# A one-layer decoder step: the order of TensorE's matmuls written by hand in the attention and HGRN2 stages

## The chip, the cores and the metric

The kernel runs on one core of a Trainium2 chip. Its engines are PE (TensorE, matrix products and transposes, which write to eight PSUM banks), DVE (VectorE), ACT (ScalarE), POOL (GpSimd) and SP (SyncE, which here issues transfers); each goes through its own instructions in order and waits on semaphores for the others. The metric is the device time of one execution in microseconds, as the median of several.

## What is computed

One layer for 256 prompt tokens and 8 sample sequences of 4 tokens (288 tokens), width 2048:

```python
sh1, sc1, ga1, sh2, sc2, ga2 = _adaln(c, w_ada, b_ada)      # silu(c) @ w_ada: the modulations
h = _rmsnorm(x, n1) * (1.0 + sc1) + sh1
q, k, v, hq, hk, hi, log_f, hg = _project(h, w_in, qg, kg, lb)
a = _attn_finish(attend(q, k, v, lam), subln_g, lam_init)   # differential attention
o_hg, s_new = _hgrn2(hq, hk, hi, log_f, s0)                 # gated linear recurrence, chunks of 64
m = _hgrn2_finish(o_hg, hg, hg_g)
x = x + ga1 * (jnp.concatenate([a, m], axis=-1) @ w_out)
h2 = _rmsnorm(x, n2) * (1.0 + sc2) + sh2
x = x + ga2 * _hier_moe(h2, ...)                            # 4 groups of 4 experts
```

For the sample tokens `attend` reads a paged cache of 2048 past keys and values for each sequence; for the prompt it is causal attention over 256 tokens. All data is float32.

## The kernel before

The program is one stream of Python that records instructions; a scheduler then puts them in an order on each engine, by what it holds to be ready and by priority. Where the code says `issue_after(first)`, what follows is only kept behind `first`; where it records under `keep_in_program_order`, PE's instructions stay in the order of the code. In the part that this change touches neither binds much, so the scheduler weaves single matmuls of different work into each other.

The work of the stages around the change:

- **Projections** (`by_features`, main at L545 to L552). A job takes one slab of a weight matrix (128 x 1024 values), which ACT rounds into a high part `wh` (L463) and DVE subtracts into a low part `wl` (L464), and multiplies it with the high and low parts of the tokens: 24 matmuls named `pf`, 128 x 288, in two groups of 12 (`mm3`, L467). Each job belongs to a step of `run`. The slabs of `wh` and `wl` are in a small ring.
- **Modulations** (`ada`, L386). A step loads two tiles of w_ada and makes 8 matmuls `pm`, 32 columns wide in the array (128*32), one for each quarter of the bank's partitions; 16 steps make one of the six modulations.
- **Cached attention** (`cache`, L1038), 16 items, each 4 slabs of keys and values of two sequences. Keys are turned (transposes `pkc`, L154, into one PSUM bank, `ck`, bank 5), copied by ACT or DVE in turn (`copy`, L157: tiles `kTc`, L160 and L162, three buffers), multiplied with the queries (`plc`, 128*32), weighed (softmax parts on DVE and ACT), turned (`ppc`), multiplied with the values (`poc`, 128*32), and added up on DVE.
- **HGRN2** for one head pair after the other: a tree of elementwise operations on DVE and ACT makes the tiles `X` (L794 to L799, L845, L848; two buffers) whose small products `pA` on PE give the scores inside a chunk; `near` (L837) copies from PSUM under a mask.
- **Prompt attention** in the stage before: logits `pl`, softmax on DVE and ACT, transposes `pdt`, values `po`, norm, transposes `pot`; the norm of the queries by `pqn`.

The streams are joined by `weave` (L120), which takes from several generators in proportion to their numbers of steps: in the attention stage 20 jobs and M0 = 24 modulation steps; in the stage "mid" 8 jobs, M1 = 8 modulation steps and C1 = 24 cache steps; in the stage "hgrn" H1 = 48 jobs and the other 40 of 64 cache steps; then "late", out projection and experts. `BANKS` names for each stage which PSUM banks a kind of tile takes in turn; `use` switches between them. The steps of `turning` are generators that make 8 transposes each, and `late` is a list of products that are recorded later.

Of the kernel before, what the change touches and what calls it, by code (L numbers as in the profile page):

```python
# [20 lines left out]
KC = 16  # L21
# [20 lines left out]
    "mid": {"pm": [7], "acc": [0, 1], "misc": [3, 4], "ck": [5], "cl": [6], "cp": [2]},  # L42
    "hgrn": {"pm": [7], "acc": [0, 1], "misc": [3, 4], "ck": [5], "cl": [6], "cp": [2]},
# [11 lines left out]
M0 = 24  # L55
M1 = 8
C1 = 24
# [74 lines left out]
class Step:  # L132
    def __init__(self, tc, io):
        self.tc, self.nc, self.io = tc, tc.nc, io
        self.flip = 0
        self.turns, self.nslab, self.nbank = {}, {}, {}
        self.pending, self.once = [], []
        self.in_order = False
# [9 lines left out]
    def mm(self, out, lhsT, rhs, start, stop):  # L148
        m = self.nc.tensor.matmul(out, lhsT=lhsT, rhs=rhs, start=start, stop=stop)  # L149
        return self.tc.keep_in_program_order(m) if self.in_order else m  # L150

    def tr(self, out, in_):
        n = in_.shape[0]
        t = self.nc.tensor.transpose(out, in_, self.ident[0:n, 0:n])  # L154
        return self.tc.keep_in_program_order(t) if self.in_order else t
# [230 lines left out]
    def ada(self, g):  # L386
# [7 lines left out]
        for k in range(KC):  # L394
# [6 lines left out]
            def products(h):  # L401
                for j in range(4):
                    m = self.mm(pm[32 * j:32 * j + 32, 256 * h:256 * h + 256], self.cT[:, k, :],
                                ws[h][:, 256 * j:256 * j + 256], k == 0 and h == 1, False)
                    if j == 0:
                        first = m
                return first
            with self.tc.issue_after(products(1).ins):
                products(0)
# [110 lines left out]
    def by_features(self, wname, blk, src, done):  # L520
# [9 lines left out]
        def make(hs, s, ps):  # L530
# [11 lines left out]
            def main():  # L542
                if s == 0:
                    ps.extend([self.acc("pf0"), self.acc("pf1")])
                for j in range(2):  # L545
                    for k in range(4):
                        kc = s * 4 + k
                        c0 = k * 256 + j * 128
                        self.mm3(ps[j][:, 0:NT], [x[:, c0:c0 + 128] for x in box["p"]],
                                 [hi[:, kc, :], lo[:, kc, :]], kc == 0, kc == KC - 1)  # L550
# [487 lines left out]
    def cache(self):  # L1038
# [7 lines left out]
        late = []  # L1046
        run = {}

# [30 lines left out]
        def turning(pr, s, par, pl):  # L1079


            at = pr * 32 + par * 16 + s * 4
            wk = self.pages("cache_k", (at, at + 1, at + 2, at + 3))
            kT = [None, None]
            for h in range(2):
                kT[h] = self.cc.tile([128, KV, 256], F32, tag="kTc", name="kTc", bufs=KTB)
                for k2 in range(2):
                    t = self.bank("ck", "pkc")
                    for k in range(2):
                        for q in range(2):  # L1090
                            kk = 2 * k2 + k
                            self.tr(t[:, (k * 2 + q) * 128:(k * 2 + q + 1) * 128], wk[h][:, q, kk * 128:(kk + 1) * 128])
                    self.copy(kT[h][:, 2 * k2:2 * k2 + 2, :].rearrange("p k t -> p (k t)"), t)
                yield
                if h == 0:
                    while late:
                        late.pop(0)()

            def products():
                if not pl:  # L1100
                    pl.append(self.bank("cl", "plc"))
                first = None
                for h in (1, 0):
                    for k in range(KV):
                        m = self.mm(pl[0][32 * k:32 * k + 32, h * 256:(h + 1) * 256], self.qB[:, 2 * pr + par, k, :],
                                    kT[h][:, k, :], par == 0 and h == 1, par == 1 and h == 0)
                        first = first or m
                return first
            late.append(products)

        def weigh(pr, s, pl):
# [3 lines left out]
            nc.vector.tensor_tensor_reduce(L, pl[0], self.c("bias"), 1.0, -NEG, OP.add, OP.max, mx)  # L1115
# [9 lines left out]
        def turn(L):  # L1125
            t = self.bank("cp", "ppc")
            for q in range(4):
                self.tr(t[:, q * 128:(q + 1) * 128], L[:, q * 128:(q + 1) * 128])
# [4 lines left out]
        def weighted(pr, s, half, pT, po):  # L1133

            at = pr * 32 + s * 4 + half * 2
            wv = self.pages("cache_v", (at, at + 16, at + 1, at + 17))

            def sums():
                for i in range(2):
                    q = half * 2 + i  # L1140
                    for k in range(KV):
                        r = slice(32 * k, 32 * k + 32)
                        self.mm(po[r, 0:256].rearrange("p (a d) -> p a d", a=2), pT[:, q * 128 + 32 * k:q * 128 + 32 * k + 32],
                                wv[i][:, :, k * 128:(k + 1) * 128], q == 0, q == 3)
            return sums
# [26 lines left out]
        def together(*parts):  # L1172

            first = parts[0]()
            with self.tc.issue_after(first.ins):
                for part in parts[1:]:
                    part()

        items = [(pr, s) for pr in range(NB // 2) for s in range(4)]
        pls = {i: [] for i in range(len(items) + 1)}  # L1180
        state = {}

        def update(i, al, po):
# [585 lines left out]
def body(tc, nc, io, stop=None):  # L1769
# [8 lines left out]
    def some(gen, n):  # L1778
        return islice(gen, n), n
# [112 lines left out]
```

## Time and profile before

| | us |
|---|---|
| median of 3 runs | 1487.66 |
| lowest and highest | 1479.43, 1490.71 |
| the profiled execution | 1485.84 |
| its span | 1483.9 |

The stages as the trace shows them (start of the first and of the last matmul of a kind): the start and early part to 158 us, the attention stage to 312, mid and hgrn with the cached attention to 711, late and the out projection to 942, the experts to the end. A matmul in float32 on small tiles leaves two records, so a count of records can be twice that of the instructions. A row of a timeline is start, length, engine, line, operation, output and input, array tile, shape, and how many records were run together; the length holds the pipeline's tail, so the distance of two starts is the time that a matmul takes from PE.

### The profile page before, as it was taken

How to read it: one execution, taken by the hardware profiler on the slowest of the kernel's cores; microseconds unless marked ns; L12 is line 12 of the kernel's file. 1: busy time of each engine (PE TensorE's matmuls, PEld its weight loads, DVE VectorE, ACT ScalarE, POOL GpSimd, SP SyncE). 2: the span in 40 equal slices, each digit the busy share in tenths (PEclk: the TensorE clock that was granted, in tenths of full speed). 3: DMA queues.
4: the chain of work that ended last, by engine and by line, in shares of the span. 5: the costliest groups of instructions: out<-in, count | busy, mean ns of one | idle time of the engine just before them, and what ended most of it. 6: DMA issues, size and time to landing. Idle time of an engine off the chain costs nothing. (4 is left out here: it accounts for less than half of the span.)

```text
span 1483.9 us, 30120 instructions
## 1 busy us (share of the span) xinstructions
PE 1385.3 (93%) x11808; PEld 933.0 (63%) x11808; DVE 652.4 (44%) x1569; ACT 370.3 (25%) x689; POOL 148.0 (10%) x194
## 2 busy tenths in 40 slices
PE   4889899999999989999989999999999999799997
PEld 3566677767878756887767998563535445353532
DVE  2332464564874456596364444224233241413134
ACT  3222243463443324443223432010000000000000
POOL 2000301110000032000041212001010010101011
PEclk9899999999999998999999999899999999799999
DMA  9999986777878867887989765888999999799997
GB/s 319 369 365 342 348 278 239 232 253 259 254 243 269 277 213 234 265 263 228 345 279 339 264 213 188 294 342 314 398 386 399 392 393 397 284 388 389 399 387 286
DMA packets 240808, 457.25 MB, mean 308 GB/s; under 512 B 17178, under 2 KB 84619, under 8 KB 240395
## 3 DMA queue, kind: packets, MB, share of 16 engines
q1 hardware_dynamic: 171218, 374.60, 70.7%
q10 hardware_dynamic: 66818, 74.10, 15.1%
q0 software_dynamic: 2624, 6.56, 1.4%
q8 instruction: 95, 1.56, 0.4%
q14 instruction: 53, 0.43, 0.1%
HBM read 446.94 MB, written 8.26 MB: 307 GB/s over the span
## 5 line engine op out<-in xcount | busy, mean ns | idle before, releaser
L464 DVE TENSOR_TENSOR wl<-w,wh 128x1024 fp32r<-128x1024 f32 x128 | 157.7, 1232 | 190.1 <-ACT wh L463 189.4
L149 PE MATMUL pf<-hhi,wh 128*128 128x288 f32 x640 | 201.5, 315 | 0.0
L463 ACT CAST wh<-w 128x1024 fp32r<-128x1024 f32 x128 | 133.8, 1046 | 267.9 <-PE pf L149 190.0
L149 PE MATMUL pf<-hlo,wh 128*128 128x288 f32 x640 | 199.5, 312 | 0.0
L149 PE MATMUL pf<-hhi,wl 128*128 128x288 f32 x640 | 198.6, 311 | 0.0
L149 PE MATMUL pm<-w,cT 128*32 128x128 f32 (+1 forms) x2048 | 127.2, 355 | 22.6 <-DMA w<-w_ada 21.9
L149 PEld LDWEIGHTS pf<-hhi,wh 128*128 128x128 f32 x640 | 123.2, 193 | 19.2 <-issue 16.8
L149 PEld LDWEIGHTS pf<-hlo,wh 128*128 128x128 f32 x640 | 123.3, 193 | 10.4 <-issue 9.9
L149 PEld LDWEIGHTS pf<-hhi,wl 128*128 128x128 f32 x640 | 123.3, 193 | 8.3 <-issue 7.8
L149 PE MATMUL pa<-w,hp 128*64 128x512 f32 x512 | 117.0, 612 | 6.5 <-PEq L1721 6.5
L149 PE MATMUL pu<-w,hp 128*64 128x512 f32 x512 | 117.4, 595 | 0.7 <-DMA w<-w_exp_up 0.5
L149 PE MATMUL py<-w,hidT 128*64 128x512 f32 x512 | 114.5, 595 | 1.4 <-DVE hidT L162 0.8
L149 PEld LDWEIGHTS pm<-w,cT 128*32 128x32 f32 x2048 | 60.6, 116 | 63.6 <-DMA w<-w_ada 30.4
L154 PE MATMUL pkc<-cst,w 128*128 128x128 f32 x512 | 88.7, 286 | 8.2 <-DVE kTc L162 7.0
L149 PEld LDWEIGHTS pg<-oh,h 128*128 128x128 f32 x768 | 88.4, 195 | 6.5 <-issue 6.5
L149 PE MATMUL pg<-oh,h 128*128 128x128 f32 x768 | 90.5, 279 | 0.0
L149 PEld LDWEIGHTS pu<-w,hp 128*64 128x64 f32 x512 | 38.6, 137 | 75.4 <-issue 66.8
L149 PEld LDWEIGHTS pa<-w,hp 128*64 128x64 f32 x512 | 36.9, 141 | 77.4 <-issue 71.0
L1289 POOL TENSOR_TENSOR x<-x,gt 128x512 f32<-128x512 f32 x24 | 33.1, 1381 | 518.5 <-DVE gt L1287 516.0
L149 PEld LDWEIGHTS py<-w,hidT 128*64 128x64 f32 x512 | 36.5, 137 | 72.8 <-issue 62.3
L1565 DVE SCALAR_TENSOR_TENSOR sa<-sa,cs,pu 128x512 f32<-128x512 f32 x8 | 6.0, 748 | 172.2 <-PE pu L149 172.2
L149 PE MATMUL pf<-mhi,wh 128*128 128x288 f32 x256 | 79.0, 309 | 0.0
(427 smaller groups left out, 2059.2 us busy)
## 6 DMA issues: line engine op xcount, KB each, us to landing
w<-w_ada SPq DMA_DIRECT2D x192, 512.0 KB, 6.6
w<-w_exp_gate SPq DMA_DIRECT2D x128, 512.0 KB, 10.4
w<-w_exp_up SPq DMA_DIRECT2D x128, 512.0 KB, 9.8
w<-w_exp_down SPq DMA_DIRECT2D x128, 512.0 KB, 10.5
w<-w_in ACTq DMA_DIRECT2D x96, 512.0 KB, 5.7
w<-cache_k SPq DMA_DIRECT2D x128, 256.0 KB, 3.9
w<-cache_v SPq DMA_DIRECT2D x128, 256.0 KB, 4.2
w<-w_out ACTq DMA_DIRECT2D x32, 512.0 KB, 5.3
```

Source lines behind the costliest of these rows:

```text
L149: m = self.nc.tensor.matmul(out, lhsT=lhsT, rhs=rhs, start=start, stop=stop)
L154: t = self.nc.tensor.transpose(out, in_, self.ident[0:n, 0:n])
L463: self.nc.scalar.copy(hi, x)
L464: self.nc.vector.tensor_sub(lo, x, hi.bitcast(F32))
L1289: eng.tensor_add(x, x, t[:, 0:n])
L1565: self.nc.vector.scalar_tensor_tensor(sa, sa, cs, pu, op0=OP.mult, op1=OP.mult)
```

## The change

Recording now has `queued` and `stream`: all matmuls that are recorded under `stream()` are tied to the one before them in one chain without a semaphore, so that PE gets them in the order of the code. The products of the modulations, each group of 12 projections, and every part of the cached attention are recorded so. The cached attention is rewritten in steps of one slab of keys (8 transposes into two banks, 5 and 7), four steps for each of the 16 items and a few behind the last, 69 in all: step 0 has the products of the item before's second half and the second half of sums of the one before that; step 2 the first half of both; steps 1 and 3 turn keys, and step 1 also the weights. The modulations leave the stages "mid" and "hgrn", where bank 7 is now the cache's: M0 is 32 (the attention stage has all of them), C1 is 10, the other 59 steps lie over the 48 jobs. The rings of the cache's pages have 7 buffers from "mid" on.

```diff
-    "mid": {"pm": [7], "acc": [0, 1], "misc": [3, 4], "ck": [5], "cl": [6], "cp": [2]},
-    "hgrn": {"pm": [7], "acc": [0, 1], "misc": [3, 4], "ck": [5], "cl": [6], "cp": [2]},
+    "mid": {"acc": [0, 1], "misc": [3, 4], "ck": [5, 7], "cl": [6], "cp": [2]},
-M0 = 24
-M1 = 8
-C1 = 24
+M0 = 32
+C1 = 10
+    def queued(self, m):
+        if self.in_order:
+            return self.tc.keep_in_program_order(m)
+        if self.streaming:
+            if self.streamed is not None:
+                self.tc.add_manual_dep(m.ins, self.streamed.name, mybir.DependencyInfo(
+                    mybir.DependencyClass.NoSync, mybir.DependencyReason.DATA), reason="streamed")
+            self.streamed = m.ins
+        return m
-            with self.tc.issue_after(products(1).ins):
+            with self.stream():
+                products(1)
                 products(0)
...
                 for j in range(2):
+                    with self.stream():
+                        for k in range(4):
...
+        def turned(w):
+            kT = self.cc.tile([128, KV, 256], F32, tag="kTc", name="kTc", bufs=KTB)
+            ts = [self.bank("ck", "pkc") for _ in range(2)]
+            with self.stream():
+                for k2, t in enumerate(ts):
+                    for k in range(2):
+                        for q in range(2):
+                            kk = 2 * k2 + k
+                            self.tr(t[:, (k * 2 + q) * 128:(k * 2 + q + 1) * 128], w[:, q, kk * 128:(kk + 1) * 128])
+            for k2, t in enumerate(ts):
+                self.copy(kT[:, 2 * k2:2 * k2 + 2, :].rearrange("p k t -> p (k t)"), t)
+            return kT
...
+        for i in range(n + 2):
+            w = keys(i, 0) if i < n else None
+            kT0 = kT1
+            with self.stream():
+                if 1 <= i <= n:
+                    products(i - 1, 1, kT0)
+                if i >= 2:
+                    sums(1, pT[i - 2], po[i - 2], wv[i - 2])
...
+            if i >= 2:
+                update(i - 2)
...
+            if i >= 1:
+                L[i - 1], al[i - 1] = weigh(i - 1)
+            kT0 = [turned(w[0])] if i < n else None
             yield
+            if i < n:
+                kT0.append(turned(w[1]))
+            if i >= 1:
+                pT[i - 1], po[i - 1] = turn(L[i - 1])
+                wv[i - 1] = values(i - 1, 0)
+            yield
+            w = keys(i, 1) if i < n else None
+            with self.stream():
+                if i < n:
+                    products(i, 0, kT0)
+                if i >= 1:
+                    sums(0, pT[i - 1], po[i - 1], wv[i - 1])
+            if i < n:
+                kT1 = [turned(w[0])]
+            yield
...
-                weave((s.run(heads(0, "f")), 8), some(mods, M1), some(cache, C1))
+                s.use("mid", pages=[r1] * R1 + [r2] * R2)
+                weave((s.run(heads(0, "f")), 8), some(cache, C1))
...
-                weave(some(rest, H1), (cache, 64 - C1))
+                weave(some(rest, H1), (cache, 69 - C1))
```

The first place is on PE, a block of the cached attention between two projection jobs. Before, products and sums were mixed with transposes:

```order
L149 MATMUL pf_4982<-hhi,wl 128x288
L154 MATMUL pkc<-cst,w 128x128 x4
L149 MATMUL plc<-kTc,qB 32x256 x2
L149 MATMUL poc<-w,pTc 32x256
L149 MATMUL plc<-kTc,qB 32x256 x6
L149 MATMUL poc<-w,pTc 32x256 x4
L154 MATMUL pkc<-cst,w 128x128
L149 MATMUL poc<-w,pTc 32x256 x3
L149 MATMUL pf_4982<-hhi,wh 128x288
```

Now the block is in the order of the code, here with two steps of the cache in a row and no job between them:

```order
L148 MATMUL pf_3429<-hhi,wl 128x288
L152 MATMUL pkc<-cst,w 128x128 x8
L152 MATMUL ppc<-cst,Lc 128x128 x4
L148 MATMUL plc<-kTc,qB 32x256 x8
L148 MATMUL poc<-w,pTc 32x256 x8
L152 MATMUL pkc<-cst,w 128x128 x8
L148 MATMUL pf_3428<-hhi,wh 128x288
```

The same instructions moved into whole runs of 8, and transposes no longer stand among them; between two such blocks there is a whole job of 24 `pf` in most places, and none in some.

The second place is on PE, the border of the attention stage to "mid", with the prompt's last head pair. Before, projections and a modulation step stood between the transposes `pdt`, the values `po` and what follows:

```order
L149 MATMUL pf_3911<-hhi,wh 128x288
L149 MATMUL pf_3911<-hlo,wh 128x288
L154 MATMUL pdt<-cst,L 128x128 x2
L149 MATMUL pf_3912<-hhi,wh 128x288
L154 MATMUL pdt<-cst,L 128x128 x2
L149 MATMUL pf_3912<-hlo,wh 128x288
L149 MATMUL pf_3911<-hhi,wl 128x288
L149 MATMUL po<-v,dT 128x128 x4
L149 MATMUL pm<-w,cT 32x256 x8
L149 MATMUL pf_3911<-hhi,wh 128x288
```

Now that chain stands without projections, up to the first transposes of cached keys:

```order
L148 MATMUL pl<-kT,qT 128x256 x2
L148 MATMUL pqn<-cst,qs 32x2 x4
L152 MATMUL pot<-cst,on 128x128 x2
L152 MATMUL pdt<-cst,L 128x128 x4
L148 MATMUL po<-v,dT 128x128 x4
L152 MATMUL pot<-cst,on 128x128 x2
L148 MATMUL pqn<-rdiag,cst 128x128 x2
L152 MATMUL pmt<-cst,mrow_2123 128x128 x4
L148 MATMUL pln<-ksT,qB 32x32 x6
L152 MATMUL pkc<-cst,w 128x128 x8
L152 MATMUL ppn<-cst,Lc 128x128
L152 MATMUL pkc<-cst,w 128x128 x8
```

The projections of "mid" moved behind the first `pkc`, since these are ahead of them in the chain.

The third place is on DVE, in the tree of HGRN2. Before, a copy of turned keys and a split `wl` stood every few elementwise operations:

```order
L798 TENSOR_TENSOR X<-X,hk 128x8x16
L799 TENSOR_TENSOR X<-X,hq 128x8x16
L794 TENSOR_TENSOR X<-lf 128x16x8
L795 TENSOR_TENSOR X<-lf 128x16x8
L794 TENSOR_TENSOR X<-lf 128x16x8
L162 COPY kTc<-pkc 128x512
L464 TENSOR_TENSOR wl<-w,wh 128x1024
L795 TENSOR_TENSOR X<-lf 128x16x8
L837 COPY_PREDICATED near<-cmask,pA 128x128
L794 TENSOR_TENSOR X<-lf 128x32x4
```

Now the copy stands behind the tree, with the split 30 rows ahead of it; this is the tree's end:

```order
L808 TENSOR_TENSOR X<-lf 128x128
L809 TENSOR_TENSOR X<-lf 128x128
L808 TENSOR_TENSOR X<-lf 128x128
L851 COPY_PREDICATED near<-cmask,pA 128x128
L809 TENSOR_TENSOR X<-lf 128x128
L859 TENSOR_TENSOR X<-lf 128x256 x2
L177 COPY kTc<-pkc 128x512
```

The copy moved behind 29 elementwise operations. In this place of HGRN2 51 elementwise operations lie between two splits `wl` now; in three others 56, 48 and 67; before there were never more than 34. On PE the same stretch has no projections:

```order
L152 MATMUL pkc<-cst,w 128x128 x4
L148 MATMUL pA<-X 32x32 x8
L152 MATMUL pkc<-cst,w 128x128
L148 MATMUL pA<-X 32x32 x8
L152 MATMUL pkc<-cst,w 128x128 x3
L148 MATMUL plc<-kTc,qB 32x256 x2
L148 MATMUL pA<-X 32x32 x48
L148 MATMUL pA<-hq,hk 32x32 x16
L148 MATMUL plc<-kTc,qB 32x256 x3
L148 MATMUL pA<-X 32x32 x8
L148 MATMUL plc<-kTc,qB 32x256 x3
L148 MATMUL pA<-X 32x32 x8
```

Before, `pf` matmuls of the next job stood among these; now the next job is behind the whole bunch.

## Rows read from the trace of the kernel before

**Rows 1.** The page: span, and busy time of each engine.

```profile
span 1483.9 us, 30120 instructions
...
PE 1385.3 (93%) x11808; PEld 933.0 (63%) x11808; DVE 652.4 (44%) x1569; ACT 370.3 (25%) x689; POOL 148.0 (10%) x194
```

**Rows 2.** Windows: busy us (instructions) of each engine, granted clock, DMA share, GB/s.

```profile
150.00:200.00 50.00, 46.23 (x367) 35.60 (x366) 24.92 (x54) 14.05 (x29) 11.55 (x17) 0.97 0.93 327
158.00:312.00 154.00, 146.10 (x1198) 114.51 (x1196) 80.29 (x223) 62.35 (x151) 20.85 (x25) 0.97 0.78 267
312.00:711.00 399.00, 386.91 (x3948) 301.31 (x3950) 249.95 (x733) 162.24 (x300) 30.45 (x56) 0.97 0.79 252
942.00:1484.00 542.00, 510.32 (x3088) 247.32 (x3084) 166.85 (x298) 31.70 (x54) 33.15 (x24) 0.98 0.97 363
546.00:553.00 7.00, 5.11 (x30) 2.78 (x30) 4.39 (x7) 0.58 (x1) 3.83 (x6) 0.51 0.38 115
```

**Rows 3.** Instructions by line on DVE, whole span: count, then busy us, mean ns, idle before.

```profile
L464 DVE TENSOR_TENSOR wl<-w,wh 128x1024 fp32r<-128x1024 f32 x128 | 157.7, 1232 | 190.1 <-ACT wh L463 189.4
...
L162 DVE COPY kTc<-pkc 128x512 f32<-128x512 f32 x64 | 44.0, 688 | 41.1 <-PE pkc L154 40.4 <-issue 0.5
...
L795 DVE TENSOR_TENSOR X<-lf 128x128 f32<-128x128 f32 x56 | 16.0, 285 | 0.0
```

**Rows 4.** PE's waits, 312 to 711 us: waited for, total, times, longest.

```profile
PE pkc L154 <- DVE kTc L162: 7.0, 4, 4.2
```

**Rows 5.** Timeline of PE (start, length, us), 363.5 to 368.

```profile
364.25 0.62 PE L149 MATMUL plc<-kTc,qB 128*32 128x256 f32 x4
364.71 0.59 PE L149 MATMUL poc<-w,pTc 128*32 128x256 f32 x2
...
366.96 0.40 PE L149 MATMUL pf<-hlo,wh 128*128 128x288 f32 x1
```

**Rows 6.** The same view, 597 to 602.

```profile
598.39 1.07 PE L149 MATMUL plc<-kTc,qB 128*32 128x256 f32 x16
599.28 1.05 PE L149 MATMUL poc<-w,pTc 128*32 128x256 f32 x16
600.26 0.40 PE L149 MATMUL pf<-hhi,wh 128*128 128x288 f32 x1
```

**Rows 7.** The same view, 735.5 to 739.5.

```profile
735.69 0.40 PE L149 MATMUL pf<-hhi,wh 128*128 128x288 f32 x1
735.93 0.29 PE L149 MATMUL pf<-hlo,wh 128*128 128x288 f32 x1
...
738.86 0.29 PE L149 MATMUL pf<-hhi,wl 128*128 128x288 f32 x1
739.08 0.64 PE L149 MATMUL pm<-w,cT 128*32 128x256 f32 x8
```

**Rows 8.** The same view, 290 to 314: the last head pair of the prompt.

```profile
292.88 1.13 PE L149 MATMUL pl<-kT,qT 64*128 64x256 f32 x4
...
305.20 0.38 PE L154 MATMUL pdt<-cst,L 128*128 128x128 f32 x2
...
306.63 1.16 PE L149 MATMUL po<-v,dT 128*128 128x128 f32 x8 [0.43 <-ACT dT L160]
...
310.03 0.41 PE L154 MATMUL pot<-cst,on 128*128 128x128 f32 x2
311.48 0.68 PE L149 MATMUL pqn<-rdiag,cst 32*128 32x128 f32 x4 [1.04 <-DVE rdiag L667]
```

**Rows 9.** Timeline of DVE, 405 to 421.

```profile
407.55 1.23 DVE L464 TENSOR_TENSOR wl<-w,wh 128x1024 fp32r<-128x1024 f32 x1
...
409.36 0.28 DVE L798 TENSOR_TENSOR X<-X,hk 128x128 f32<-128x128 f32 x1
409.56 0.28 DVE L799 TENSOR_TENSOR X<-X,hq 128x128 f32<-128x128 f32 x1
...
419.03 1.22 DVE L464 TENSOR_TENSOR wl<-w,wh 128x1024 fp32r<-128x1024 f32 x1
```

More of the change, by code (lines that the diff above doesn't have):

```diff
@@ L1 @@
-from contextlib import ExitStack
+from contextlib import ExitStack, contextmanager
 from itertools import islice
@@ L1045, in cache @@
         wsel = self.c("wsel").rearrange("p (a c) -> p a c", a=2)
-        late = []
         run = {}
+        kT1 = None
         def new_tokens(pr):
@@ L1077, in new_values, with keys @@
             return O
-        def turning(pr, s, par, pl):
+        def keys(i, par):
+            pr, s = items[i]
             at = pr * 32 + par * 16 + s * 4
[L1083 to L1088, printed above, removed]
+            return self.pages("cache_k", (at, at + 1, at + 2, at + 3))
+        def turned(w):
[3 more added lines that the diff above has]
+                for k2, t in enumerate(ts):
                     for k in range(2):
@@ L1091, in turning, with products, weigh @@
                             kk = 2 * k2 + k
[L1092 to L1111, printed above, removed]
+                            self.tr(t[:, (k * 2 + q) * 128:(k * 2 + q + 1) * 128], w[:, q, kk * 128:(kk + 1) * 128])
+            for k2, t in enumerate(ts):
+                self.copy(kT[:, 2 * k2:2 * k2 + 2, :].rearrange("p k t -> p (k t)"), t)
+            return kT
+        def products(i, par, kT):
+            pr, s = items[i]
+            if par == 0:
+                pls[i] = self.bank("cl", "plc")
+            for h in (1, 0):
+                for k in range(KV):
+                    self.mm(pls[i][32 * k:32 * k + 32, h * 256:(h + 1) * 256], self.qB[:, 2 * pr + par, k, :],
+                            kT[h][:, k, :], par == 0 and h == 1, par == 1 and h == 0)
+        def weigh(i):
+            pr, s = items[i]
             m, tot = run[pr]
@@ L1131, in turn, with values, sums @@
             return pT, self.bank("cp", "poc")
-        def weighted(pr, s, half, pT, po):
+        def values(i, half):
+            pr, s = items[i]
             at = pr * 32 + s * 4 + half * 2
[L1136 to L1145, printed above, removed]
+            return self.pages("cache_v", (at, at + 16, at + 1, at + 17))
+        def sums(half, pT, po, wv):
+            for i in range(2):
+                q = half * 2 + i
+                for k in range(KV):
+                    r = slice(32 * k, 32 * k + 32)
+                    self.mm(po[r, 0:256].rearrange("p (a d) -> p a d", a=2), pT[:, q * 128 + 32 * k:q * 128 + 32 * k + 32],
+                            wv[i][:, :, k * 128:(k + 1) * 128], q == 0, q == 3)
         def finish(pr, O):
@@ L1170, in finish, with update @@
                                      t[:, 0:128].rearrange("p (b h t) -> p b h t", b=4, h=8), AF.Copy, scale=self.subln)
[L1172 to L1177, printed above, removed]
         items = [(pr, s) for pr in range(NB // 2) for s in range(4)]
-        pls = {i: [] for i in range(len(items) + 1)}
+        n = len(items)
+        pls, al, L, pT, po, wv = {}, {}, {}, {}, {}, {}
         state = {}
-        def update(i, al, po):
+        def update(i):
             pr, s = items[i]
             O = state["O"]
-            nc.vector.scalar_tensor_tensor(O, O, al, po[:, 0:256].rearrange("p (a d) -> p a d", a=2),
+            nc.vector.scalar_tensor_tensor(O, O, al[i], po[i][:, 0:256].rearrange("p (a d) -> p a d", a=2),
                                            op0=OP.mult, op1=OP.add)
```

87 lines of the change are left out of this document (33 added, 54 removed).

## The prediction

> **What bounds the kernel now.** I read the page first for the busy shares: PE has work for 1385.3 of 1483.9 us, DVE for 44% and ACT for 25% [rows 1]. So PE's order is the place where time can go or come, and the other engines matter where PE waits for them. The windows by stage say more: from 312 to 711 us, where the change does most, PE is busy 386.91 of 399 us and DVE 249.95; the DMA share is 0.79 [rows 2]. A gain there has to be PE work made shorter, since only 12 us are idle. From 942 on the DMA share is 0.97 at 363 GB/s with PE busy 510.32 of 542 [rows 2]; nothing of that stretch is touched, and I let it shift as a whole, so a gain or loss ahead of it passes to the end. The waits of PE come third: the longest group in 312 to 711 is that of the transposes `pkc` for the copy `kTc`, 7.0 us in 4 waits, one of them 4.2 [rows 4].
>
> The sum is made against the profiled execution, 1485.84 us, which is 0.1% under the median of 1487.66.
>
> **What becomes shorter.** A block of the cached attention is 8 `plc` and 8 `poc`, 32 records. Where `plc` and `poc` are mixed it takes from 364.25 to the next `pf` at 366.96, 2.71 us [rows 5]; where both are whole, from 598.39 to 600.26, 1.87 us [rows 6]. The difference is 0.84 us. Of the 32 blocks before, some 25 stand broken in PE's order; nearly all are whole after. 25 x 0.84 = 21 us. The price is not the same in each broken block, so I keep 12 to 25.
>
> The second part is the number of changes between the whole array and strips of 32 columns. A job of 24 `pf` between two visits to the strips takes from 735.69 to 739.08, 3.39 us, though its matmuls follow each other by 0.133 (738.86 less 735.93, over 22) [rows 7]: 24 x 0.133 = 3.19, and 0.20 us is the price of one visit. Outside the blocks PE's order has 56 runs of HGRN2's small products `pA` before and 27 after, and 114 and 87 runs of other kinds: 56 visits fewer, 11 us (8 to 13).
>
> The third is waits. With two banks for turned keys the wait for the one bank should go, 7.0 us [rows 4]; and after the longest one the granted clock was 0.51 from 546 to 553, that is 1.2 instead of 2.4 GHz [rows 2], a loss of about half of 7 us. Both together are 10.5; some of it will be found elsewhere, so I take 8 (2 to 10).
>
> Together 21 + 11 + 8 = 40 us, with 22 to 48 as bounds.
>
> The Trainium skill speaks against half of that: its page "TensorEngine Tiling (Array Packing)", Key Properties, says that changing the tiling mode drains the array and that changing only the tile does not. Products and sums of the cache are both 128*32, so by this rule a block that is mixed only of these two costs one visit like a whole one, and the 21 us would be near nothing. The row of the mixed block disagrees, since there is no other mode between 364.25 and 366.96 and the block is 0.84 us longer; I go by the row.
>
> **What becomes longer.** (1) The border of the attention stage to "mid". Before, the last pair of prompt heads has its logits `pl` at 292.88, the transposes `pdt` at 305.20, the values `po` at 306.63, `pot` at 310.03 and the last `pqn` at 311.48 [rows 8]: 18.6 us of softmax, copies and norm on ACT, DVE and POOL, in which PE had `pf` and modulation steps to run (the second place of the change, before). After, nothing but this chain's own transposes and products stands on PE from these logits up to the first `pkc` (the second place of the change): the projections of "mid" are behind the cache's transposes in the written chain, and these take a bank that the prompt attention gives back. What PE does itself there is about 3 us, and ACT and DVE have less to do between, so the chain is nearer 16 than 18.6: 13 us idle (8 to 17). (2) HGRN2's tree. `X` has two buffers, so DVE and PE go through it in step. Before, one split `wl` to the next with the tree between took from 407.55 to 419.03, 11.5 us [rows 9], and PE's waits in that whole stage stayed small [rows 4], since `pf` of the next jobs stood in the gaps. After, four places have 51, 56, 48 and 67 elementwise operations between two splits, and the copies `kTc` for which PE's chain is waiting (0.69 us each [rows 3]) are queued behind them, as are the splits that the next jobs need. One such operation takes from 0.20 us (409.36 to 409.56 [rows 9]) to 0.285 [rows 3]; 222 of them take 44 to 63 us, and I take 60, since larger copies are among them. PE has in each place one job of 3.4 us and some 6.6 us of small products and transposes: 40 in all. 60 - 40 = 20 us idle. The low bound is 5 (44 us of operations, PE's work as now), the high one 35 (63 us, and half of the jobs not yet free to run). Queued behind the waiting product on PE is all the rest of the projections, and behind them the casts `wh` on ACT, since the ring of parts is short. (3) 69 steps over 56 jobs put two steps against each other in some 12 places: the product waits for a copy that has only just been begun, 0.69 us [rows 3]: 12 x 0.5 = 6 us (3 to 9). (4) The ends of the items, which have no projection among their small products: 3 us (0 to 4). (5) Eight more modulation steps in the attention stage: 8 x 1 MB (two tiles of 128 x 1024 values each) on top of the 267 GB/s x 154 us = 41 MB that it moves now; 49 MB in the 164 us that it then lasts is 302 GB/s, under the 327 that 150 to 200 has at a share of 0.93 [rows 2]. Most of it is hidden: 3 us (0 to 8). The PE work of these steps is moved, not added. (6) The clock. The one wait of 4.2 us brought 7 us at half rate [rows 2, 4]; five idle stretches of 4 to 13 us will bring some of that: 6 us (0 to 17).
>
> Together 13 + 20 + 6 + 3 + 3 + 6 = 51 us, with 16 to 90 as bounds if all went one way.
>
> Elsewhere the count of instructions is the same. Taking the second bank costs nothing on its own, since the modulations that held bank 7 no longer run in these stages; if some did, a whole stage would stand.
>
> **Sum.** 1485.84 - 40 + 51 = 1496.8, say 1497 us, 0.6% above the median: the gain of the written order is real, and the stalls that a written order can't fill take it back.
>
> **Rivals.** *The stalls are mostly covered* (faster): DVE runs ahead in the tree during the job before it, because its data are ready, and the copies `kTc` that ACT takes come in time. Then item 2 is 5, the clock costs 0 and the border 8: 40 gained, 5 + 8 + 6 + 3 + 3 = 25 lost, 1471 us. For it: DVE is busy 63% of 312 to 711 [rows 2]; against it: two buffers of `X`. It decides from where the four places idle less than 5 us together. *The stalls in full* (slower): item 2 at 35, the border at 17, the clock at 10, the rest 9 (some of items 3 to 5 hidden in these): 71 against 40, 1517. For it: every projection is queued behind the chain. *Blocks gain nothing* (slower): a mixed block is only as long as what it waits for, and whole blocks wait as long; the gain is 19 in place of 40, 51 are lost, 1518. Against it stands the row of the whole block at 1.87 us in the same stage. The rule of "TensorEngine Tiling (Array Packing)", Key Properties, in the Trainium skill gives this case. *Nothing that counts* (same): what PE saves is found as idle time at once, since the transfers and the copies set the pace; 1486.
>
> **How the numbers follow.** Chances: forecast 0.40, covered stalls 0.26, stalls in full 0.16, no gain in blocks 0.10, nothing 0.08. The forecast's own range is 1476 to 1515: the single terms are uncertain by 5 to 15 us each, in both directions. A measurement of this kernel can tell about 1%, that is 1473 to 1502.5, from no change. Faster: the covered case nearly whole and a little of the forecast, 0.26. Slower: stalls in full, no gain in blocks, and a fifth of the forecast, 0.34. Same: the rest, 0.40. Range for 8 in 10: 1458 to 1522, from the lower part of the covered case to just above the two slower ones.
>
> **What would show it.** In the profile after: blocks of 16 + 16 records at 1.87 us, and 24 `pf` between them, show the gain; a gap of 10 us or more between the last `po` of the prompt and the first `pkc` shows item 1; waits of `plc` and `pkc` for `kTc` of DVE of 15 us or more in the four trees, with DVE busy without a gap there, show item 2; granted clock near 0.5 behind these shows item 6. The prediction is wrong if PE's waits for `kTc` and `X` add up to under 5 us, or if whole blocks are not shorter than broken ones.

## The result, and the profile after

The changed kernel takes 1535.99 us (median of 4 runs, 1523.81 to 1538.62) beside 1489.18 us for the kernel before (4 runs, 1479.43 to 1491.04): 1.0312 times as long, 95% interval 1.0240 to 1.0384. The forecast was 1497 us with a range to 1522; the time lies above it, and above the 1517 and 1518 us of the two slower rivals. The profiled execution took 1536.82 us at a granted clock of 0.931; the four executions lie between 0.931 and 0.943.

The page of the changed kernel, its span, PE's share and PE's granted clock in 40 slices (tenths of full speed):

```profile
span 1534.9 us, 30120 instructions
...
PE 1394.7 (91%) x11808; PEld 952.5 (62%) x11808; DVE 648.7 (42%) x1569; ACT 370.0 (24%) x687; POOL 145.0 (9%) x194
...
PEclk9889999879879997988997999799999999999999
```

PE's busy time is nearly that of before [rows 1]: 1394.7 against 1385.3 us, in a span that is 51 us longer. The clock shows where to look: nine of the slices from the eighth to the 26th stand at 7 or 8.

To compare the stages I take the stretch from the last projection by tokens to the last weighted values of the cache, which holds the same projections and the same cache work in both kernels (they differ by 18 records of modulations and 4 of projections, under 1 us). The windows of before and of after, with busy us (records) of PE, PEld, DVE, ACT and POOL, the granted clock, the DMA share and GB/s:

```profile
158.10:710.60 552.50, 532.50 (x5139) 415.46 (x5137) 330.23 (x955) 224.19 (x450) 51.20 (x81) 0.97 0.79 256
```

```profile
161.50:755.20 593.70, 532.95 (x5123) 427.98 (x5122) 328.58 (x956) 224.43 (x449) 49.53 (x80) 0.90 0.73 241
```

The stretch is 41 us longer, with the same busy time of PE, and that same busy time hides two opposite changes. Idle is length less busy: 20 us before, 61 after. The trace's records of the clock, summed over these stretches, have 30.7 us at half rate before and 116.1 after; 2.1 and 26.2 us of it fall on idle time, and I reckon half of the rest, 14 and 45 us, as what matmuls lost. So PE's work reckoned at full clock is 532.5 - 14 = 518 us before and 533 - 45 = 488 after. The written order does save 30 us of PE's work, and 41 us of idle and 31 us of half clock take its place: -30 + 41 + 31 = 42, the 41 us but for rounding. The halving is an estimate, and a little high: at half rate the projections from 321.19 to 322.15 us follow each other by 0.24 us, 1.8 times the 0.133 of [rows 7]. With 1.8 in place of 2 the gain and the loss by the clock are 27 us each. Of the span's 51 us another 6 lie behind the stretch and 3 ahead of it.

The waits of PE in this stretch of after, total us, times, longest:

```profile
PE pA L148 <- DVE X L813: 13.2, 10, 2.5
PE pdt L152 <- DVE L L728: 4.4, 1, 4.4
PE pkc L152 <- ACT kTc L175: 4.4, 4, 3.3
...
PE pot L152 <- DVE on L757: 3.3, 4, 2.3
PE plc L148 <- ACT kTc L175: 3.0, 4, 1.5
PE pkc L152 <- DVE kTc L177: 2.9, 4, 1.1
PE pSs L148 <- DVE st L1004: 2.8, 3, 2.4
PE plc L148 <- DVE kTc L177: 2.6, 4, 0.8
```

Before, the longest of such groups in the same stages was 7.0 us [rows 4]; that wait of `pkc` for one bank is down to 2.9 for DVE's copies, and most of the other places are new (`pSs` had 2.6 us before).

The border of the attention stage, on PE (start, length; in brackets idle before and what ended it):

```profile
297.62 1.13 PE L148 MATMUL pl<-kT,qT 64*128 64x256 f32 x4
299.78 0.59 PE L148 MATMUL pqn<-cst,qs 128*32 128x2 f32 x8 [1.03 <-DVE L L712]
300.72 0.66 PE L152 MATMUL pot<-cst,on 128*128 128x128 f32 x2 [0.35 <-DVE on L757]
305.81 1.11 PE L152 MATMUL pdt<-cst,L 128*128 128x128 f32 x4 [4.43 <-DVE L L728]
307.60 2.08 PE L148 MATMUL po<-v,dT 128*128 128x128 f32 x8 [0.68 <-ACT dT L175]
311.99 0.66 PE L152 MATMUL pot<-cst,on 128*128 128x128 f32 x2 [2.30 <-DVE on L757]
313.44 1.19 PE L148 MATMUL pqn<-rdiag,cst 32*128 32x128 f32 x4 [0.79 <-DVE rdiag L681]
...
317.06 1.30 PE L152 MATMUL pkc<-cst,w 128*128 128x128 f32 x5 [0.25 <-PE pln L148]
```

This answers to [rows 8]: from `pl` at 297.62 to the first `pkc` at 317.06 are 19.4 us, and no projection stands between. The gaps of 1.03, 0.35, 4.43, 0.68, 2.30 and 0.79 us add up to 9.6, and behind `pl` the operations are longer than before by a factor of 1.6 to 1.8: `po` x8 takes 2.08 us to the 1.16 of [rows 8], `pot` 0.66 to 0.41, the last `pqn` 1.19 to 0.68. (The view ends at 318 us, so the last row has 5 of the 8 `pkc`.)

The first tree of HGRN2, on PE and then on DVE:

```profile
395.86 0.64 PE L148 MATMUL pA<-X 128*32 128x32 f32 x32 [0.33 <-DVE X L813]
398.52 1.81 PE L148 MATMUL pA<-X 128*32 128x32 f32 x64 [2.02 <-DVE X L813]
400.75 0.66 PE L148 MATMUL pA<-hq,hk 128*32 128x32 f32 x32 [0.42 <-DVE near L851]
402.21 1.08 PE L148 MATMUL plc<-kTc,qB 128*32 128x256 f32 x6 [0.80 <-DVE kTc L177]
...
407.99 1.10 PE L152 MATMUL pkc<-cst,w 128*128 128x128 f32 x8
408.84 0.38 PE L148 MATMUL pf<-hhi,wh 128*128 128x288 f32 x1
```

```profile
393.88 1.23 DVE L477 TENSOR_TENSOR wl<-w,wh 128x1024 fp32r<-128x1024 f32 x1 [0.59 <-ACT wh L476]
...
401.47 0.68 DVE L177 COPY kTc<-pkc 128x512 f32<-128x512 f32 x1
...
404.61 0.30 DVE L851 COPY_PREDICATED near<-cmask,pA 128x128 f32<-128x128 uint8 x1 [1.05 <-PE pA L148]
```

PE waits 0.33, 2.02, 0.42 and 0.80 us for the tree's results and for a copy of keys, and at 408.84 comes the first projection since 392.6. On DVE the copy `kTc` at 401.47 stands behind the tree's operations that began after the split at 393.88, as the order had shown; the wait at 398.52 was for `X` itself.

A block of the cache, where it is whole:

```profile
476.16 1.07 PE L148 MATMUL plc<-kTc,qB 128*32 128x256 f32 x16
477.04 1.05 PE L148 MATMUL poc<-w,pTc 128*32 128x256 f32 x16
478.02 1.09 PE L152 MATMUL pkc<-cst,w 128*128 128x128 f32 x8
```

`plc` and `poc` take 478.02 - 476.16 = 1.86 us, the price of [rows 6]; before, a mixed one took 2.71 [rows 5].

### The profile page after: what moved, and what is told of

It reads as the page before. It is cut to its first block, busy times and chain, and to the rows that moved or that the text cites. A ratio compares the mean times of both kernels' runs of the same rounds, so it can differ in the third digit from the quotient of the medians.

```text
span 1534.9 us, 30120 instructions
## 1 busy us (share of the span) xinstructions
PE 1394.7 (91%) x11808; PEld 952.5 (62%) x11808; DVE 648.7 (42%) x1569; ACT 370.0 (24%) x687; POOL 145.0 (9%) x194
## 5 line engine op out<-in xcount | busy, mean ns | idle before, releaser
L148 PE MATMUL pf<-hhi,wl 128*128 128x288 f32 x640 | 195.4, 305 | 0.0
L148 PE MATMUL pm<-w,cT 128*32 128x128 f32 (+1 forms) x2048 | 122.7, 357 | 16.8 <-DMA w<-w_ada 16.2
L152 PE MATMUL pkc<-cst,w 128*128 128x128 f32 x512 | 76.2, 290 | 7.6 <-ACT kTc L175 4.4
```

The source lines that it names most:

```text
L148: return self.queued(self.nc.tensor.matmul(out, lhsT=lhsT, rhs=rhs, start=start, stop=stop))
L152: return self.queued(self.nc.tensor.transpose(out, in_, self.ident[0:n, 0:n]))
```

## The experiments

Each run is a kernel of its own, timed against the kernel before on the same chip; ratios are to that. "Idle" and "half clock" are of the same stretch as above, the first from the window's length less PE's busy time.

**e1: the projections outside the chain.**

```diff
-                    with self.stream():
-                        for k in range(4):
+                    for k in range(4):
```

> The changed kernel with one part undone: the groups of 12 projections are no longer in the written chain; modulations and all parts of the cached attention still are. In PE's order products and sums of the cache stay whole (25 of 32 blocks of sums, 17 of products), the projections run 165 times instead of 79 and stand among HGRN2's small products again, and DVE has at most 32 tree operations between two splits. Theory 1 (the loss is idle time that the projections can't fill because they are in the chain, and the half clock that follows it): PE's idle between 160 and 760 us falls from 55 to about 20, half clock from 119 us to about 35, and the time falls by 45 to 65 us, to 1470 to 1490 (at most as before, or under it by the whole blocks). Theory 2 (the loss is in the cache's own steps, two against each other, or in the moved modulations): the time stays above 1515.

Measured: 1475.95 us, ratio 0.9923 (0.9892 to 0.9955). The window of the stretch:

```profile
160.70:697.10 536.40, 514.37 (x5154) 409.36 (x5152) 327.58 (x956) 224.25 (x451) 50.56 (x80) 0.98 0.80 266
```

536.4 us in place of 593.7, with 22 us idle and the granted clock at 0.98 (20.5 us at half rate). Theory 1 holds: with one line undone, 60 us of the change go, and the rest of the change is 0.8% faster than the kernel before. PE's work at full clock is 506 us here, 18 more than in the changed kernel: the projections in the chain save that much, and pay 39 us of idle time and 36 of half clock for it.

**e2: two jobs ahead of the cache's first step.**

```diff
-                weave((s.run(heads(0, "f")), 8), some(cache, C1))
+                fj = s.run(heads(0, "f"))
+                for _ in islice(fj, 2):
+                    pass
+                weave((fj, 6), some(cache, C1))
```

> The changed kernel with two projection jobs of the next stage recorded ahead of the first cache step, so that 48 projections stand in the chain ahead of the first turned keys and can run during the last prompt heads' softmax. Nothing else is moved. Theory 1: of the 10 us idle at this border half or more goes, and part of the 24 us at half clock around it: 8 to 20 us shorter, 1516 to 1528. Theory 2 (the border is hidden by what comes after): no change that can be told, 1530 to 1540.

Measured: 1524.63 us, ratio 1.0265 (1.0212 to 1.0319), 11 us under the changed kernel; the two intervals overlap, so this difference isn't settled. The trace is of the fastest of the four executions (1516.07 to 1533.71 us). The window:

```profile
160.80:736.10 575.30, 518.60 (x5122) 418.85 (x5122) 328.81 (x956) 226.66 (x451) 49.54 (x80) 0.93 0.74 247
```

Idle is 57 us, only 4 less than in the changed kernel: the 48 projections moved up to the last logits, and the gaps ahead of `pdt` (4.6 us) and `pot` (2.2) stayed. Half clock in the stretch fell from 116 to 78.5 us, and the stretch is 18 us shorter, but most of that is not shown to come from the edit: 17 of the 38 us at half rate stood at 165 to 292 us of the changed kernel's trace, ahead of the border, and 10 more at 572 to 585, far behind it. At the border itself half rate fell from 23.9 to 17.1 us. The median lies in theory 1's range; the experiment leaves open whether the border is worth that much.

**e3: the copies of turned keys at high priority.**

```diff
-                self.copy(kT[:, 2 * k2:2 * k2 + 2, :].rearrange("p k t -> p (k t)"), t)
+                with self.tc.high_priority(offset=PRIO):
+                    self.copy(kT[:, 2 * k2:2 * k2 + 2, :].rearrange("p k t -> p (k t)"), t)
```

> The changed kernel with the copies of turned keys recorded at high priority, as the splits are. In DVE's order at most 33 tree operations in three of the four trees lie between two splits now (66 in one), and on PE three of the four trees' products have projections around them again; one stretch without projections stays. Theory 1a (what starves PE is the copy queued behind the tree): idle at the trees falls from about 22 to about 8 us, half clock there from 48 to about 20 us: 20 to 30 us shorter, 1506 to 1516. Theory 1b (PE waits for the tree's X whatever the copies do): within 8 us of 1536.

Measured: 1529.88 us, ratio 1.0291 (1.0235 to 1.0347): theory 1b by the time, and neither by the trace. PE's waits in the stretch:

```profile
PE ppc L152 <- ACT Lc L1131: 12.8, 5, 4.1
...
PE pA L148 <- DVE X L813: 2.9, 4, 2.0
```

The waits for `X` fell from 13.2 to 2.9 us, so the copies did hold the chain at the trees. What took their place is the chain's next link, the weights that PE turns (`ppc`), 12.8 us where there had been 2.2. Once one late part of the chain was moved ahead, another was late.

**e4: the kernel before with the modulations moved.**

```diff
-M0 = 24
-M1 = 8
+M0 = 32
+M1 = 0
```

> The kernel before with only the modulations moved: all 32 steps of the two modulations lie in the attention stage, none in the next (M0 = 32, M1 = 0); no written order, one bank. Theory 1: the work is only moved, and the transfers of the attention stage still fit: within 5 us of before, 1484 to 1494. Rival: the attention stage is bound by w_ada then, and part of the 47 us is lost here: 8 us or more above before.

Measured: 1482.75 us, ratio 0.9974 (0.9948 to 1.0001). The transfers of the attention stage fit, the rival falls.

**e5: two chains.** The projections are tied to each other in a chain of their own, everything else as in the change.

```diff
-            if self.streamed is not None:
+            last = self.streamed.get(self.streaming)
+            if last is not None:
...
-            self.streamed = m.ins
+            self.streamed[self.streaming] = m.ins
...
-                    with self.stream():
+                    with self.stream("pf"):
```

> The changed kernel with two written chains in place of one: the projections are tied to each other in a chain of their own, the modulations and the cache's parts in the other; no projection is tied to a part of the cache. In PE's order projections have 166 runs between the first turned keys and the last sums (79 in the changed kernel), and the longest stretch without any is 6 us by count (11.5). Theory 1 (the harm is that projections wait behind cache parts in ONE chain): as with the projections outside the chain, 1468 to 1484. Rival (tying projections to each other in writing is harmful by itself, since a late split then holds all later ones): 1500 or more.

Measured: 1478.92 us, ratio 0.9942 (0.9907 to 0.9977). Writing the order of projections costs nothing that can be told; tying them to the cache's parts does.

**e6: the cache outside the chain.** Projections and modulations stay in one chain; `turned`, `products`, `sums` and `turn` are in none.

```diff
-    def stream(self):
-        was, self.streaming = self.streaming, True
+    def stream(self, name=None):
+        was, self.streaming = self.streaming, name
...
-            with self.stream():
+            with self.stream("pf"):
                 products(1)
...
-                    with self.stream():
+                    with self.stream("pf"):
                         for k in range(4):
```

> The changed kernel with the other half undone: projections and modulations are in a chain, the parts of the cached attention (keys, products, sums, weights) are in none. The rewritten steps alone still leave 17 to 19 of 32 blocks whole in PE's order. Theory 1: any of the two halves outside the chain lets projections fill the waits: 1470 to 1490, and near the kernel with projections outside (1476). Rival (the written order of projections against modulations is what costs): above 1505.

Measured: 1485.37 us, ratio 0.9990 (0.9950 to 1.0029). Theory 1 again, though 9 us behind e1; e7 shows where.

**e7: the kernel before with projections and modulations in one chain.** The modulations are moved as in e4; the cache is the old one.

```diff
+            with self.stream():
+                products(1)
+                products(0)
-            with self.tc.issue_after(products(1).ins):
-                products(0)
...
                 for j in range(2):
+                    with self.stream():
+                        for k in range(4):
-                    for k in range(4):
```

> The kernel before with the modulations all in the attention stage (M0 = 32, M1 = 0) and a written chain of projections and modulations alone; the cache's steps are the old ones, in one bank. Blocks of the cache stay broken (5 or 6 of 32 whole). Theory 1: as the same kernel without the chain (1482.75), within 6 us; together with the run that has the cache outside of the chain it tells what the rewritten steps and the second bank bring alone: 5 to 12 us if whole blocks are worth 0.84 us each for 13 blocks more. Rival: a chain on projections costs 10 us or more here too.

Measured: 1494.28 us, ratio 1.0046 (1.0014 to 1.0078), 11 us above e4, where I expected at most 6: by the time this is the rival's sign. The stretch to the last cache values is the same to 1 us in both (544.9 and 545.6); the difference comes behind it, where modulations and projections of the out projection are in one chain. One wait there, in the kernel with two chains, in the changed kernel, and in this one (total us, times, longest):

```profile
PE pi L148 <- DVE st L1005: 1.8, 3, 0.7
```

```profile
PE pi L148 <- DVE st L1004: 4.4, 3, 3.3
```

```profile
PE pi L150 <- DVE st L1007: 4.0, 3, 2.9
```

In the three kernels that have modulations and projections in one chain (the changed one, e6, e7) the state's products `pi` wait 4.0 to 4.4 us, in e5 and in the kernel before 1.8. The part behind the last cache values lasts 779 to 782 us in these three traces and 771 to 775 in those of the kernel before, e1, e4, e5 and e9. Of the changed kernel's 47 us some 6 lie here.

e7 has the same chain as e6 and the old cache steps in one bank, so the two also show what the rewritten steps and the second bank bring by themselves: 9 us of the medians, within the 5 to 12 expected, though the intervals overlap a little. In the traces' stretches PE goes through 344 changes of array mode in e7 and 341 in e6, and 3 and 17 or so of the 32 blocks have all 16 records of a kind in one run; PE's work reckoned at full clock is 521 and 506 us. So PE's work became shorter where the changes of mode stayed the same in number: 14 blocks more at 0.84 us would be 12 of the 15 us. Not all need be the blocks', since the transposes of keys stand in longer runs too (98 in place of 155). The stretch itself is only 3 us shorter in e6, since idle time takes 5 us back and half clock 7.

**e8: two chains, copies first.** e5 with the edit of e3.

> Two chains as in the run before it, and the copies of turned keys at high priority. Products and sums are whole in 19 and 26 of 32 blocks, projections have 159 runs. Theory 1: with projections to fill the waits, an earlier copy is worth little: within 5 us of the kernel with two chains. Rival: copies still decide, 8 us or more faster than with two chains.

Measured: 1477.47 us, ratio 0.9918 (0.9886 to 0.9950), the same as e5: with projections free to fill the waits, earlier copies bring nothing that can be told.

**e9: no chain at all.**

```diff
-        if self.streaming:
+        if False:
             if self.streamed is not None:
```

> The changed kernel without any written order: the rewritten steps of the cache, the second bank and the moved modulations stay, nothing is tied to anything. 18 of 32 blocks are whole in PE's order, projections have 169 runs between the first turned keys and the last sums. Theory 1: no chain, no stalls; the rewritten steps alone bring what the kernel with only projections outside the chain has, less the better order of the cache: 1474 to 1486. Rival (the chain of the cache itself brings the gain): 1488 or more.

Measured: 1479.35 us, ratio 0.9963 (0.9932 to 0.9993). So the rewritten steps with their second bank and the moved modulations are worth 0.4% alone, with an interval that ends just under 1, and the chain on the cache (e1) adds about as much again; the two intervals overlap, and I can't part them.

**e10: a longer wait.** The changed kernel with ACT copying the weights onto themselves 8 times an item, before PE turns them.

```diff
             nc.scalar.activation(al, m2, AF.Exp, bias=m, scale=-1.0)
+            for _ in range(8):
+                nc.scalar.copy(L, L)
```

> The changed kernel with one wait made longer on purpose: behind the exponentials of each of the cache's 16 items ACT copies the weights onto themselves 8 times (about 0.6 us each, 4.7 us an item) before they are turned. PE has the same instructions in nearly the same order; the transposes of the weights stand in the chain with the projections behind them. It measures what a wait in the chain costs together with the half clock behind it. Theory 1: of 16 x 4.7 = 75 us some 20 to 45 us are idle time on PE, and each us of idle brings another 0.5 to 1 us by half clock: 1565 to 1615. Rival (the job of projections between covers it, 3.4 us of the 4.7): 1536 to 1550.

Measured: 1639.95 us, ratio 1.1041 (1.1015 to 1.1066), above what I expected. Window and wait:

```profile
163.60:865.40 701.80, 558.18 (x5122) 451.14 (x5121) 331.18 (x956) 297.97 (x577) 49.50 (x80) 0.85 0.61 204
```

```profile
PE ppc L152 <- ACT Lc L1133: 88.9, 15, 9.6
```

All of the added time is exposed, and some more: ACT is busy for 73.5 us more (298.0 in place of 224.4), and idle is 144 us, 83 more than in the changed kernel, so nothing between the weighing and the turning had been to spare. Half clock is 208 us, 92 more; that costs 27 us by the sum above, a third of a us for each us of idle, less than I had put.

**e13: the longer wait, filled.** e10 with 40 transposes of the identity in the chain ahead of the weights' own four; nothing reads them.

```diff
             with self.stream():
+                for q in range(40):
+                    self.tr(t[:, q % 4 * 128:(q % 4 + 1) * 128], self.ident)
                 for q in range(4):
```

> The kernel with the longer weighing, and PE kept at work in that wait: 40 transposes of the identity into the same bank stand in the chain ahead of the weights' own four, 16 x 40 x 0.109 = 70 us of work at full clock that nothing reads. The wait for the weights stays as long. If the half clock comes from PE standing idle, half clock between 160 us and the last sums falls from 208 to under 130 us and idle from 143 to under 90, and the time does not rise although PE has 70 us more to do: 1590 to 1640. If the half clock has another cause (the load of the other engines, the transfers), the 70 us come on top in part and half clock stays above 180: 1650 or more.

Measured: 1631.32 us, ratio 1.0966 (1.0910 to 1.1023): the median is 9 us less than that of e10, with some 70 us more for PE to do. The intervals of the two ratios just overlap, so the 9 us aren't settled; that the time did not rise is.

```profile
158.90:844.40 685.50, 604.76 (x5762) 497.67 (x5761) 330.39 (x956) 297.98 (x577) 50.76 (x80) 0.91 0.62 209
```

```profile
PE ppc L152 <- ACT Lc L1133: 25.2, 10, 6.3
```

Half clock fell from 208 to 123 us, idle from 144 to 81, the wait for the weights from 88.9 to 25.2. In the four executions of each the granted clock is 0.912 to 0.919 in e10 and 0.934 to 0.940 here. So PE's own idleness brings the half clock that e10 added: where useless work took its place the clock stayed up, with the same copies ahead of the turning and the same work on the other engines.

**e11 and e12: a kernel that beats both.** e1 with one cache step for each job of the first stage; e12 has the copies first besides.

```diff
-C1 = 10
+C1 = 8
```

> The kernel with the projections outside the chain, and C1 = 8 in place of 10: in the first stage of the cache one step to each of the 8 jobs, 61 steps over the other 48. In PE's order 30 of 32 blocks of sums and 21 of products are whole, projections have 136 runs (165). Theory 1: fewer broken blocks and visits at 0.84 and 0.2 us: 3 to 10 us under 1476, that is 1466 to 1473. Rival: blocks and visits are worth nothing here, 1474 to 1480.

Measured: 1467.85 us, ratio 0.9904 (0.9883 to 0.9926).

```profile
157.40:689.00 531.60, 507.94 (x5155) 406.97 (x5154) 324.99 (x956) 225.43 (x451) 50.77 (x80) 0.99 0.81 269
```

The trace is of the fastest of the five executions (1457.85 us). It has 508 us of busy time in 531.6, a clock of 0.99: at full clock PE's work is 501 us, 5 less than in e1, as the order's 30 whole blocks of sums (25 in e1) and 136 runs of projections (165) let expect; the intervals of e1 and e11 overlap, so the 8 us between their medians are not settled.

> As the run before it, and the copies of turned keys at high priority: 22 and 27 whole blocks, 130 runs of projections. Theory 1: within 4 us of the run before it, since projections fill the waits for copies; rival: 5 us or more faster.

Measured: 1471.23 us, ratio 0.9909 (0.9879 to 0.9939): no difference to e11.

## Why the prediction was wrong

**The gain was right.** 25 blocks at 0.84 us and 56 visits at 0.20 made 32 us; PE's work at full clock fell by 30, or 27 with the factor of 1.8. Whole blocks take 1.86 us after. Both counts were somewhat high: by the traces' records 6 or 7 of the 32 blocks are whole before and 28 or so after (24 of `plc` and 21 of `poc` in one run of 16 records, most of the others in 14 or 15), and PE has 141 and 93 runs in strips of 32 columns, 48 fewer. The rival that blocks gain nothing falls with that and with e6 and e7, where 14 blocks more are whole at the same number of changes of mode. The Trainium skill says in "TensorEngine Tiling (Array Packing)", Key Properties, that a change of tiling mode drains the array and a change of the tile alone does not. By that rule only the visits would have been left, some 11 us; by the measured 27 to 30, and by the 15 between e7 and e6, the row was the better guide here.

**The waits that were to go** were put at 8 us with their half clock. Of PE's waits for copies of keys the 7.0 us for DVE became 2.9, but 4.4 for ACT's copies and 5.6 of `plc` for either came: together 13 us where there had been 8 with ACT's; the term was in truth a loss of about 5 us, part of it what item 3 had forecast.

**The idle time was right in total, too large in one place and spread otherwise.** Items 1 to 5 made 45 us; idle rose by 41, 8 us of removed waits not taken off. The border has 9.6 us (13 forecast, 8 to 17). The trees have 13.2 for `X` with some us for copies and `near` beside it, 15 to 18 (20 forecast, 5 to 35). The mechanism differs in a part: I had PE wait at the trees for copies behind the tree, and named 15 us or more of waits of `plc` and `pkc` for DVE's `kTc` as its sign; these are 5.5. The trace shows PE waiting for `X`, and e3 shows the copy as the first cause, since PE had nothing else once the chain stood. For the modulations I took 3 us; the attention stage shows no wait for w_ada after, and e4 a gain if anything.

**The step that failed is item 6, the clock.** It stood at 6 us (0 to 17) and measured 31 in the stretch. I had one example, a wait of 4.2 us with 7 us at half rate behind it [rows 2, 4], and gave five stretches a part of that, since I counted the stretch behind a wait alone. The windows of the changed kernel over the border and the trees show what really happens:

```profile
298.00:323.00 25.00, 14.69 (x76) 11.73 (x75) 9.88 (x45) 6.62 (x23) 4.42 (x8) 0.52 0.27 79
397.00:408.00 11.00, 8.09 (x161) 4.76 (x161) 8.64 (x34) 3.15 (x5) 1.26 (x4) 0.53 0.37 127
431.00:453.00 22.00, 15.11 (x249) 10.88 (x244) 17.41 (x79) 6.31 (x14) 1.55 (x6) 0.61 0.33 100
667.00:678.00 11.00, 6.54 (x147) 6.21 (x148) 10.38 (x38) 4.08 (x8) 1.46 (x4) 0.53 0.20 66
700.00:712.00 12.00, 8.33 (x180) 6.93 (x180) 9.07 (x37) 3.11 (x5) 1.15 (x4) 0.57 0.22 72
```

The clock is 0.52 to 0.61 in them (at or near 1.2 of 2.4 GHz, but for the ends of the windows, the first 4 us at 431 above all): not one long wait followed by a recovery, but 11 to 25 us of small gaps and short matmuls (PE busy for 14.69 of 25 us at the border, 8.09 of 11 in the first tree), with the clock down almost to the end. At the border the half rate lasts 24 us for 9.6 us of idle time. These five windows hold 72 of the 116 us at half rate. The other 44 us (30.7 in all before) fall on stretches in which PE is nearly always busy, with waits of some us ahead of them, the longest from 571.72 to 585.37 us without any idle time in it.

e13 shows the cause in e10, and that the half clock comes and goes with the projections in the chain does not hang on one trace: the granted clock is 0.931 to 0.943 in the four executions of the changed kernel and 0.953 to 0.972 in all those of e1, e5, e6 and e9. With 31 in place of 6 the forecast's own sum would have been 1522. Over the whole span the same reckoning gives 42 us of idle time more (140.2 in place of 98.6), 44 us of half clock more and 35 us of PE's work less, together 51 (39 and 30 for the last two with the factor of 1.8). The forecast had 45 - 8, 6 and 32. So the clock makes 33 to 38 of the 40 us that it was short of the profiled execution.

**The ends.** I had let everything behind the cache shift as a whole. It took 6 us more, which the chain of modulations and projections brings (e6, e7). Waits explain little of it: `pi` waits 2.6 us longer, but idle time there is 46.6 us in place of 45.5. Half rate is 68.9 us in place of 43.5, by the halving 11 us of loss, and PE's work at full clock comes out 6 us less, which I can't explain; the halving is no finer than that. The 3 us ahead of the stretch lie in a part that differs by as much between runs (its end is at 157.4 to 163.8 us in the kernels above, which share it).

**Covered stalls**, the faster rival, hung on DVE running ahead in the tree. It doesn't, in the changed kernel; e1 shows that projections outside the chain cover the tree: no wait for `X` is among its nine longest groups of waits (4.1 to 0.8 us).

## What to carry to other kernels

A written order on the engine that bounds the kernel saves what it says, but it takes from the engine the work that it could do while one link is late; tie together what must be contiguous, and leave the bulk work untied or in a chain of its own. When idle time is to be added to TensorE, count with it the half clock over the whole thinned stretch, not only over the gaps: here 31 us for 41, and 27 for 83 where single longer waits were added (e10). In e3 moving one late link ahead only showed the next one.

## What the runs showed of the hardware

The granted clock stood near half rate through whole stretches of small matmuls with gaps between them (25 us at 0.52), the matmuls in them too, not only behind a long wait. Useless transposes in the 16 waits for the weights raised the clock of the stretch from 0.85 to 0.91, so that a kernel with 70 us more work on PE took no longer (1631 us to 1640). Mixing two kinds of products costs PE time inside one array mode too: 2.71 us in place of 1.87 for 32 records [rows 5, 6], and e7 and e6, with 344 and 341 changes of mode in the stretch, have 521 and 506 us of PE's work there.
